# Differential attention on Trainium2: both maps' scores in one five-bank tile, a block's products with v in one bank

## The chip, the core and the metric

One Trainium2 chip, of which the program uses one core. The time is the device time of one execution of the whole program in microseconds (us); a kernel's figure is the median of several executions. The engines are PE (TensorE, matmuls; PEld is its loading of weights), DVE (VectorE), ACT (ScalarE), POOL (GpSimd) and SP (SyncE, which issues transfers). Matmuls write to PSUM, which has eight banks of 512 float32 columns over 128 partitions; DVE and ACT read it from there. The granted clock of PE is given as a share of its full 2.4 GHz: 1.00 is that level and 0.50 is 1.2 GHz.

## The reference

The program runs two layers of a hybrid model over 1024 latent tokens and 256 context tokens. In each layer one projection feeds three groups of heads (differential attention, windowed attention, a recurrent unit), whose outputs are joined by an output projection; a gated MLP follows. The change concerns differential attention alone. It has four heads with two maps each, of 32 dimensions, and values of 64:

```python
def attend(qb, keys, vals):
    s = jnp.einsum('bqhmd,bkhmd->bhmqk', qb, keys).astype(F32) * scale
    p = jax.nn.softmax(s, axis=-1)
    w = p[:, :, 0] - lam * p[:, :, 1]
    return jnp.einsum('bhqk,bkhd->bqhd', w.astype(vals.dtype), vals)
```

Latent queries see all 1280 keys, context queries (layer 0 only) the 256 keys of the context. The result is normalised per head.

## The kernel before

`phase_b` (L699) runs windowed attention and then `da` (L860), once per layer. `da` works through units: a head of one pair of heads, with a block of query tiles of 128 tokens (four tiles of latents, or the two context tiles). Each tile of a unit is a step. Layer 0 has 40 steps, of which 32 are long (1280 keys) and 8 short (256 keys); layer 1 has 32 long ones. So there are 72 steps and 144 maxima.

A long step does, for each of the two maps: three score matmuls into a PSUM tile of three banks (512, 512 and 256 columns, L901, `da_s`), the negated maximum over the keys on DVE (L911), and the exponential with its sum on ACT (L918, `da_e`; the sum is read out by a second instruction, ACTIVATION_READ_ACCUMULATOR). `combine` then forms the weights of both maps on DVE: a reciprocal (L929), a small product (L930), and one wide operation that adds the scaled map 1 to map 0 (L931). Ten transposes on PE (L942, `da_t`) follow, in groups of 4, 4 and 2, which ACT copies out (L943, `da_w`, two of 512 columns and one of 256), and ten pairs' worth of products with v (`pv_mm`, L742, `da_pv`), which use the upper and lower half of the partitions in turn. `pv_combine` (L744) adds the halves: a copy on ACT (L749, `pvt`) and an addition on DVE (L750, `da_o`), once for each step. After a block's second head, `sub_norm` normalises it in three instalments.

Eight PSUM banks are shared out as follows: the pool psD has two buffers of a score tile (six banks), so that the two maps of a step have one each; the pool of `ps_t` has two banks, which transposes, products with v and all fill work take in turn.

Fill work stands between the steps. `fill_plan` (L1008) spreads over them parts of the output projection (`piece`: nine matmuls of 426, 428 or 342 columns, L1048 to L1050, `oy_ps`; a scaled copy on ACT, L1054, `oy_z`; an addition on POOL, L1056) and of the modulation of later stages (`mod_units`: matmuls L302, a copy on ACT L330, transposes L291, sums on DVE L293 and L296). There are 24 pieces in either layer.

The kernel states operations in a written order, but a scheduler sets the order on each engine when the program is built, and sees to the waits; where a PSUM tile is concerned it does so by banks. In each engine the instructions then run in that order. The source of `da` states for step n: combination n−1, products n−2, the maxima and exponentials of n, `finish` n−2, fill, the scores of n+1 with the transposes n−1 between the two maps.

Of the kernel before, what the change touches and what calls it, by code (L numbers as in the profile page):

```python
# [11 lines left out]
F32 = mybir.dt.float32  # L12
F32R = mybir.dt.float32r
AF = mybir.ActivationFunctionType
ALU = mybir.AluOpType
AX = mybir.AxisListType
PSUM = bass.MemoryType.PSUM
# [4 lines left out]
P = 128  # L22
NLAT = 1024
NCTX = 256
T = NLAT + NCTX
# [145 lines left out]
class Build:  # L171
# [527 lines left out]
    def phase_b(self):  # L699
        nc, tc = self.nc, self.tc  # L700
        with ExitStack() as st:
            self.sp = st.enter_context(tc.tile_pool(name="sB", bufs=1))
            self.s5_bufs = 6
            todo = [(1, nb) for nb in range(6, 12)] if self.last else \
                [(0, nb) for nb in range(4, 12)] + [(1, nb) for nb in range(6)]
            self.lambdas()
            with tc.tile_pool(name="psS", bufs=3, space=PSUM) as pss:
                v = self.load_v(256)
                loaded = [self.sw_in, self.sw_load(1, "h")]
                for g in range(2):  # L710
                    self.sw(pss, v, *loaded[g], g)
            with tc.tile_pool(name="psD", bufs=2, space=PSUM) as pss:
                self.da(pss, todo)

    def lambdas(self):
# [144 lines left out]
    def da(self, pss, todo):  # L860

        nc, sp = self.nc, self.sp
        loaded = [{}, {}]
        self.yh, self.yl, self.ld = {}, {}, {}

        def load(pair, ms):
            if 0 in ms:
                loaded[pair]["v"] = self.load_v(P * pair)  # L870
            for m in ms:
                loaded[pair][m] = self.da_load(pair, m)

        load(0, (0, 1))
        load(0, (2, 3))
        blocks = ([] if self.last else [([8, 9], 8)]) + [([0, 1, 2, 3], 0), ([4, 5, 6, 7], 0)]
        units = []
        for pair in range(2):
            bs = [dict(pair=pair, tiles=tiles, kt0=kt0, nk=10 - kt0, nkc=T - P * kt0, nqb=P * len(tiles))
                  for tiles, kt0 in blocks]  # L880
            for hd in range(2):
                for blk in bs:
                    units.append(dict(blk=blk, hd=hd))
        steps = [(u, ti) for u in units for ti in range(len(u["blk"]["tiles"]))]
        ns = len(steps)
        state = [dict(e=[], s=[None, None]) for _ in steps]
        plan = self.fill_plan(ns, todo)
        late = []

        def scores(n, mi):  # L890
            u, ti = steps[n]
            b = u["blk"]
            nkc = b["nkc"]
            t = b["tiles"][ti]
            tok = slice(P * t, P * t + P)
            qm, km = loaded[b["pair"]][2 * u["hd"] + mi]
            k0 = T - nkc
            s = state[n]["s"][mi] = pss.tile([P, T], F32, tag="s", name="da_s")
            for c in range(0, nkc, 512):
                w = min(512, nkc - c)  # L900
                nc.tensor.matmul(s[:, c:c + w], qm[:, tok], km[:, k0 + c:k0 + c + w], start=True, stop=True)  # L901

        def maximum(n, mi):
            u, ti = steps[n]
            st, b = state[n], u["blk"]
            if mi == 0:
                st["sm"] = sp.tile([P, 8], F32, tag="sm", name="da_sm", bufs=8)
                if u["hd"] == 0 and ti == 0:
                    b["s0"] = sp.tile([P, 4, 2, 2], F32, tag="s0", name="da_s0", bufs=5)
                    b["o"] = self.s5("da_o")  # L910
            nc.vector.tensor_reduce(st["sm"][:, mi:mi + 1], st["s"][mi][:, :b["nkc"]], AX.X, ALU.max, negate=True)  # L911

        def exps(n, mi):
            u, ti = steps[n]
            st, b = state[n], u["blk"]
            nkc = b["nkc"]
            e = self.x_tile("da_e")
            nc.scalar.activation(e[:, :nkc], st["s"][mi][:, :nkc], AF.Exp, bias=st["sm"][:, mi:mi + 1],  # L918
                                 accum_out=b["s0"][:, ti, u["hd"], mi:mi + 1])
            st["e"].append(e)  # L920

        def combine(n):

            u, ti = steps[n]
            st, b = state[n], u["blk"]
            sm, (w, e1) = st["sm"], st["e"]
            s01 = b["s0"][:, ti, u["hd"], :]
            nkc = b["nkc"]
            nc.vector.reciprocal(sm[:, 4:5], s01[:, 1:2])  # L929
            nc.vector.scalar_tensor_tensor(sm[:, 5:6], s01[:, 0:1], self.nlam, sm[:, 4:5], ALU.mult, ALU.mult)  # L930
            nc.vector.scalar_tensor_tensor(w[:, :nkc], e1[:, :nkc], sm[:, 5:6], w[:, :nkc], ALU.mult, ALU.add)  # L931

        def transpose(n):
            u, ti = steps[n]
            st, b = state[n], u["blk"]
            w = st["e"][0]
            wt = st["wt"] = self.wt_tile("da_w", F32)
            for c in range(0, b["nk"], 4):
                n4 = min(4, b["nk"] - c)
                pt = self.ps_t("da_t")  # L940
                for i in range(n4):
                    nc.tensor.transpose(pt[:, P * i:P * i + P], w[:, P * (c + i):P * (c + i) + P], self.ident)  # L942
                nc.scalar.activation(wt[:, P * c:P * (c + n4)], pt[:, :P * n4], AF.Copy)  # L943

        def products(n):
            u, ti = steps[n]
            st, b = state[n], u["blk"]
            hd, nk = u["hd"], b["nk"]
            pv = st["pv"] = self.ps_t("da_pv")[:, :P]
            for c in range(nk):  # L950
                self.pv_mm(pv, c, nk, loaded[b["pair"]]["v"][:, b["kt0"] + c, 64 * hd:64 * hd + 64],
                           st["wt"][:, P * c:P * c + P])

        def finish(n):
            u, ti = steps[n]
            b = u["blk"]
            self.pv_combine(u["hd"], state[n]["pv"], b["o"][:, P * ti:P * ti + P], P)
            if u["hd"] == 1 and ti == len(b["tiles"]) - 1:
                late.append(self.sub_norm(b))

        scores(0, 0)
        scores(0, 1)
        for n in range(ns + 2):
            if n == ns // 4 + 3:
                load(1, (0, 1))
            if n == ns // 2 + 3:
                load(1, (2, 3))
            if n == ns - 10:
                for k in range(2, KE):
                    self.y_load(k, "h")  # L970
            if n == ns - 4:
                self.y_split(2, nc.scalar, nc.gpsimd)
            if n == ns - 3:
                self.y_split(3, nc.scalar, nc.gpsimd)
            prev, new, out = 1 <= n <= ns, n + 1 < ns, n >= 2
            if prev:
                combine(n - 1)
            if out:
                products(n - 2)
            if n < ns:  # L980
                maximum(n, 0)
            if n < ns:
                exps(n, 0)
            if n < ns:
                maximum(n, 1)
            if n < ns:
                exps(n, 1)
            if out:
                finish(n - 2)
            if n < ns:  # L990
                for fn in plan[n]:
                    fn()
            if new:
                scores(n + 1, 0)
            if prev:
                transpose(n - 1)
            if new:
                scores(n + 1, 1)
            late = [g for g in late if next(g, True) is None]
            if n == ns - 2:  # L1000
                self.wo = [self.weight(self.a["wo"][self.l, 0], KE * P)]
        for fn in plan[ns]:
            fn()
        for g in late:
            for _ in g:
                pass
# [763 lines left out]
```

## Time and profile before

| | |
|---|---|
| median of the runs | 3106.06 us (3 runs: 3099.3, 3106.1, 3106.06) |
| the profiled execution | 3104.49 us, its span 3102.6 us |
| granted clock of PE, mean | 0.972 |
| busy over the whole span | PE 2845.3 us (92%), DVE 2109.1 (68%), ACT 1457.5 (47%) |
| maxima L911, 144 of them | 195.5 us busy |
| exponentials L918, 144 | 177.5 us busy |
| scores L901, 400 | 125.2 us busy |

The span is the time from the first to the last instruction of one execution. A row of the timeline gives an instruction's start, its duration, and in brackets how long the engine was idle before it and what ended that; a row marked x2 or more stands for instructions that ran without a gap. Differential attention takes from about 488 to 727 us in layer 0 and from 2121 to 2327 us in layer 1.

### The profile page before, as it was taken

How to read it: one execution, taken by the hardware profiler on the slowest of the kernel's cores; microseconds unless marked ns; L12 is line 12 of the kernel's file. 1: busy time of each engine (PE TensorE's matmuls, PEld its weight loads, DVE VectorE, ACT ScalarE, POOL GpSimd, SP SyncE). 2: the span in 40 equal slices, each digit the busy share in tenths (PEclk: the TensorE clock that was granted, in tenths of full speed). 3: DMA queues.
4: the chain of work that ended last, by engine and by line, in shares of the span. 5: the costliest groups of instructions: out<-in, count | busy, mean ns of one | idle time of the engine just before them, and what ended most of it. 6: DMA issues, size and time to landing. Idle time of an engine off the chain costs nothing. (4 is left out here: it accounts for less than half of the span.)

```text
span 3102.6 us, 41077 instructions
## 1 busy us (share of the span) xinstructions
PE 2845.3 (92%) x15194; PEld 2307.3 (74%) x15194; DVE 2109.1 (68%) x2979; ACT 1457.5 (47%) x2442; POOL 1497.3 (48%) x971
## 2 busy tenths in 40 slices
PE   6899798999899999998988989798989799998898
PEld 4798665667688888887877778666767678887676
DVE  6956577875855444457887875767885755555997
ACT  5444367775444333343322454467873444444331
POOL 4645402223455444439561664602323566665981
PEclk9999899999999999999999999899999999999999
DMA  7232816654121121143215331454434122224322
GB/s 251 83 93 68 202 27 228 204 197 149 59 80 67 67 75 67 67 174 118 82 57 206 92 108 52 123 121 146 134 110 166 55 82 82 82 82 163 121 84 82
DMA packets 207577, 349.27 MB, mean 113 GB/s; under 512 B 32784, under 2 KB 112400, under 8 KB 207376
## 3 DMA queue, kind: packets, MB, share of 16 engines
q1 hardware_dynamic: 202768, 331.69, 33.2%
q0 software_dynamic: 4608, 14.95, 2.2%
q8 instruction: 120, 1.97, 0.3%
q14 instruction: 81, 0.66, 0.1%
HBM read 257.19 MB, written 89.39 MB: 112 GB/s over the span
## 5 line engine op out<-in xcount | busy, mean ns | idle before, releaser
L184 ACT ACTIVATE w_r<-w_raw 128x512 fp32r<-128x512 f32 x338 | 212.7, 631 | 449.7 <-PE u_ps L1518 280.1
L1490 POOL TENSOR_TENSOR w_raw<-w_raw 128x512 f32<-128x512 f32 x176 | 250.3, 1427 | 227.5 <-DVE w_r L187 102.8
L187 DVE TENSOR_TENSOR w_r<-w_raw,w_r 128x512 fp32r<-128x512 f32 x206 | 150.4, 732 | 251.5 <-ACT w_r L184 251.4
L187 POOL TENSOR_TENSOR w<-raw,w 128x1024 fp32r<-128x1024 f32 (+2 forms) x62 | 142.9, 2311 | 318.2 <-ACT w L184 207.1
L1517 PE MATMUL u_ps<-a,w_r 128*128 128x512 f32 x704 | 278.6, 396 | 5.3 <-DVE vb L1605 4.2
L1518 PE MATMUL u_ps<-a,w_r 128*128 128x512 f32 x704 | 277.8, 395 | 1.4 <-DVE a L187 1.2
L1519 PE MATMUL u_ps<-a,w_r 128*128 128x512 f32 x704 | 276.2, 392 | 0.0
L187 POOL TENSOR_TENSOR w_r<-w_raw,w_r 128x512 fp32r<-128x512 f32 x132 | 190.4, 1442 | 119.9 <-ACT w_r L184 114.7
L1369 PE MATMUL d_ps<-d_ah,d_b 128*128 128x512 f32 x560 | 223.1, 399 | 22.5 <-DVE xd L1346 11.1
L1370 PE MATMUL d_ps<-d_al,d_b 128*128 128x512 f32 x560 | 222.8, 398 | 9.0 <-DVE d_al L187 9.0
L1371 PE MATMUL d_ps<-d_ah,d_b 128*128 128x512 f32 x560 | 221.8, 396 | 0.7 <-DVE d_b L187 0.7
L911 DVE TENSOR_REDUCE da_sm<-da_s 128x1 f32<-128x1280 f32 (+1 forms) x144 | 195.5, 1368 | 34.1 <-PE da_s L901 32.7
L918 ACT ACTIVATE da_e<-da_s,da_sm 128x1280 f32<-128x1280 f32 (+1 forms) x144 | 177.5, 1235 | 23.7 <-DVE da_sm L911 20.6
L1056 POOL TENSOR_TENSOR oy_x<-oy_x,oy_z 128x426 f32<-128x426 f32 (+3 forms) x48 | 52.7, 1099 | 223.5 <-ACT oy_z L1054 191.7
L1517 PEld LDWEIGHTS u_ps<-a,w_r 128*128 128x128 f32 x704 | 133.8, 190 | 35.0 <-DVE vb L1605 5.7
L1518 PEld LDWEIGHTS u_ps<-a,w_r 128*128 128x128 f32 x704 | 133.9, 190 | 29.5 <-DVE a L187 2.0
L1519 PEld LDWEIGHTS u_ps<-a,w_r 128*128 128x128 f32 x704 | 133.7, 190 | 28.7
L1346 DVE SCALAR_TENSOR_TENSOR xd<-d_ps,mods,xd 128x512 f32<-128x512 f32 x200 | 141.0, 740 | 20.4 <-PE d_ps L1371 20.3
L1369 PEld LDWEIGHTS d_ps<-d_ah,d_b 128*128 128x128 f32 x560 | 107.6, 192 | 48.5 <-issue 9.4
L901 PE MATMUL da_s<-dak,daq 96*128 96x512 f32 (+1 forms) x400 | 125.2, 399 | 17.6 <-ACT da_e L918 17.4
L1605 DVE TENSOR_TENSOR vb<-u_ps,vb 128x512 f32<-128x512 f32 x96 | 66.1, 688 | 98.7 <-PE u_ps L1519 89.1
L1370 PEld LDWEIGHTS d_ps<-d_al,d_b 128*128 128x128 f32 x560 | 108.0, 193 | 32.0 <-DVE d_al L187 10.3
(347 smaller groups left out, 8635.6 us busy)
## 6 DMA issues: line engine op xcount, KB each, us to landing
wmod<-in_wmod SPq DMA_DIRECT2D x96, 512.0 KB, 6.4
w_raw<-in_wu SPq DMA_DIRECT2D x44, 1024.0 KB, 5.4
d_w<-in_wd SPq DMA_DIRECT2D x40, 512.0 KB, 3.9
d_a<-ud SPq DMA_DIRECT2D x40, 512.0 KB, 4.7
ud<-conv SPq DMA_DIRECT2D x22, 640.0 KB, 2.9
ud<-conv SPq DMA_DIRECT2D x22, 512.0 KB, 2.6
raw<-in_wg SPq DMA_DIRECT2D x16, 512.0 KB, 4.3
dak<-qk_da POOLq DMA_DIRECT2D x48, 160.0 KB, 8.1
```

The lines of the kernel that those rows point to most:

```text
L184: self.nc.scalar.activation(out, in_, AF.Copy)
L187: (eng or self.nc.vector).tensor_tensor(out, in_, hi.bitcast(F32), ALU.subtract)
L911: nc.vector.tensor_reduce(st["sm"][:, mi:mi + 1], st["s"][mi][:, :b["nkc"]], AX.X, ALU.max, negate=True)
L918: nc.scalar.activation(e[:, :nkc], st["s"][mi][:, :nkc], AF.Exp, bias=st["sm"][:, mi:mi + 1], accum_out=b["s0"][:, ti, u["hd"], mi:mi + 1])
L1346: nc.vector.scalar_tensor_tensor(x, ps, gate, x, ALU.mult, ALU.add)
L1369: nc.tensor.matmul(ps, bh[:, w], ah[:, m], start=on is None and k == 0, stop=False, **kw)
L1370: nc.tensor.matmul(ps, bh[:, w], al[:, m], start=False, stop=False, **kw)
L1371: nc.tensor.matmul(ps, bl[:, w], ah[:, m], start=False, stop=k == 1, **kw)
L1490: sub = lambda o, a, b, op=ALU.subtract: nc.gpsimd.tensor_tensor(o, a, b, op)
L1517: nc.tensor.matmul(ps, wh[:, s], h, start=new and kk == 0, stop=False, skip_group_check=not new)
L1518: nc.tensor.matmul(ps, wh[:, s], lo, start=False, stop=False, skip_group_check=not new)
L1519: nc.tensor.matmul(ps, wl[:, s], h, start=False, stop=kk == 3, skip_group_check=not new)
```

## The change

The pool psD has one buffer instead of two, and holds two tiles. `both` has 2560 columns, which are five banks: map 0 in columns 0 to 1279, map 1 in columns 1280 to 2559. Its third bank (columns 1024 to 1535) holds the end of map 0 and the beginning of map 1. The score matmuls of map 1 are cut at 256 and 768 so that each stays in one bank. The tile `pv` is one bank, in which up to four tiles of a unit put their products with v, 128 columns each; `pv_combine` then runs once for each unit, over 256 or 512 columns: 20 times instead of 72. The source states the maxima and exponentials of step n ahead of combination n−1, `finish` ahead of the scores, and the scores in two parts around the fill.

```diff
@@ -709,7 +709,7 @@
                 loaded = [self.sw_in, self.sw_load(1, "h")]
                 for g in range(2):
                     self.sw(pss, v, *loaded[g], g)
-            with tc.tile_pool(name="psD", bufs=2, space=PSUM) as pss:
+            with tc.tile_pool(name="psD", bufs=1, space=PSUM) as pss:
                 self.da(pss, todo)
 
     def lambdas(self):
@@ -883,11 +884,16 @@
                     units.append(dict(blk=blk, hd=hd))
         steps = [(u, ti) for u in units for ti in range(len(u["blk"]["tiles"]))]
         ns = len(steps)
-        state = [dict(e=[], s=[None, None]) for _ in steps]
+        state = [dict(e=[]) for _ in steps]
+        both = pss.tile([P, 2 * T], F32, tag="s", name="da_s")
         plan = self.fill_plan(ns, todo)
         late = []
 
-        def scores(n, mi):
+        def score(n, mi):
+            b = steps[n][0]["blk"]
+            return both[:, T * mi:T * mi + b["nkc"]]
+
+        def scores(n, mi, parts):
             u, ti = steps[n]
             b = u["blk"]
             nkc = b["nkc"]
@@ -895,10 +901,12 @@
             tok = slice(P * t, P * t + P)
             qm, km = loaded[b["pair"]][2 * u["hd"] + mi]
             k0 = T - nkc
-            s = state[n]["s"][mi] = pss.tile([P, T], F32, tag="s", name="da_s")
-            for c in range(0, nkc, 512):
-                w = min(512, nkc - c)
-                nc.tensor.matmul(s[:, c:c + w], qm[:, tok], km[:, k0 + c:k0 + c + w], start=True, stop=True)
+            cuts = [0, 512, 1024, nkc] if mi == 0 else [0, 256, 768, nkc]
+            s = score(n, mi)
+            for i in parts:
+                c, e = cuts[i], min(cuts[i + 1], nkc)
+                if c < e:
+                    nc.tensor.matmul(s[:, c:e], qm[:, tok], km[:, k0 + c:k0 + e], start=True, stop=True)
 
         def maximum(n, mi):
             u, ti = steps[n]
@@ -908,14 +916,14 @@
                 if u["hd"] == 0 and ti == 0:
                     b["s0"] = sp.tile([P, 4, 2, 2], F32, tag="s0", name="da_s0", bufs=5)
                     b["o"] = self.s5("da_o")
-            nc.vector.tensor_reduce(st["sm"][:, mi:mi + 1], st["s"][mi][:, :b["nkc"]], AX.X, ALU.max, negate=True)
+            nc.vector.tensor_reduce(st["sm"][:, mi:mi + 1], score(n, mi), AX.X, ALU.max, negate=True)
 
         def exps(n, mi):
             u, ti = steps[n]
             st, b = state[n], u["blk"]
             nkc = b["nkc"]
             e = self.x_tile("da_e")
-            nc.scalar.activation(e[:, :nkc], st["s"][mi][:, :nkc], AF.Exp, bias=st["sm"][:, mi:mi + 1],
+            nc.scalar.activation(e[:, :nkc], score(n, mi), AF.Exp, bias=st["sm"][:, mi:mi + 1],
                                  accum_out=b["s0"][:, ti, u["hd"], mi:mi + 1])
             st["e"].append(e)
 
@@ -946,7 +954,9 @@
             u, ti = steps[n]
             st, b = state[n], u["blk"]
             hd, nk = u["hd"], b["nk"]
-            pv = st["pv"] = self.ps_t("da_pv")[:, :P]
+            if ti == 0:
+                u["pv"] = pss.tile([P, 512], F32, tag="pv", name="da_pv")
+            pv = u["pv"][:, P * ti:P * ti + P]
             for c in range(nk):
                 self.pv_mm(pv, c, nk, loaded[b["pair"]]["v"][:, b["kt0"] + c, 64 * hd:64 * hd + 64],
                            st["wt"][:, P * c:P * c + P])
@@ -954,12 +964,13 @@
         def finish(n):
             u, ti = steps[n]
             b = u["blk"]
-            self.pv_combine(u["hd"], state[n]["pv"], b["o"][:, P * ti:P * ti + P], P)
-            if u["hd"] == 1 and ti == len(b["tiles"]) - 1:
-                late.append(self.sub_norm(b))
-
-        scores(0, 0)
-        scores(0, 1)
+            if ti == len(b["tiles"]) - 1:
+                self.pv_combine(u["hd"], u["pv"], b["o"], b["nqb"])
+                if u["hd"] == 1:
+                    late.append(self.sub_norm(b))
+
+        for mi in range(2):
+            scores(0, mi, range(3))
         for n in range(ns + 2):
             if n == ns // 4 + 3:
                 load(1, (0, 1))
@@ -973,29 +984,26 @@
             if n == ns - 3:
                 self.y_split(3, nc.scalar, nc.gpsimd)
             prev, new, out = 1 <= n <= ns, n + 1 < ns, n >= 2
+            if n < ns:
+                maximum(n, 0)
+                exps(n, 0)
+                maximum(n, 1)
+                exps(n, 1)
             if prev:
                 combine(n - 1)
             if out:
                 products(n - 2)
-            if n < ns:
-                maximum(n, 0)
-            if n < ns:
-                exps(n, 0)
-            if n < ns:
-                maximum(n, 1)
-            if n < ns:
-                exps(n, 1)
-            if out:
                 finish(n - 2)
+            if new:
+                scores(n + 1, 0, (0, 1))
             if n < ns:
                 for fn in plan[n]:
                     fn()
             if new:
-                scores(n + 1, 0)
+                scores(n + 1, 0, (2,))
+                scores(n + 1, 1, range(3))
             if prev:
                 transpose(n - 1)
-            if new:
-                scores(n + 1, 1)
             late = [g for g in late if next(g, True) is None]
             if n == ns - 2:
                 self.wo = [self.weight(self.a["wo"][self.l, 0], KE * P)]
```

How the emitted order changes. In these rows a name ending in a number is one of several buffers; the number behind [waits ...] is that of a semaphore, and the word ahead of it the engine or queue waited for (Activation is ACT).

On DVE, in long steps of layer 0, before (da_s_4447 are the sums of the exponentials):

```order
L931 SCALAR_TENSOR_TENSOR da_e<-da_e,da_sm 128x1280 [waits DVE_49]
L911 TENSOR_REDUCE da_sm<-da_s 128x1 [waits PE_49]
L929 RECIPROCAL da_sm<-da_s_4447 128x1 [waits Activation_49]
L750 TENSOR_TENSOR da_o<-da_pv,pvt 64x128 [waits Activation_49]
L930 SCALAR_TENSOR_TENSOR da_sm<-da_s_4447,nlam,da_sm 128x1 [waits DVE_49]
L911 TENSOR_REDUCE da_sm<-da_s 128x1 [waits PE_49]
L931 SCALAR_TENSOR_TENSOR da_e<-da_e,da_sm 128x1280 [waits DVE_49]
L911 TENSOR_REDUCE da_sm<-da_s 128x1 [waits PE_49]
```

The same place now:

```order
L919 TENSOR_REDUCE da_sm<-da_s 128x1 [waits PE_49]
L919 TENSOR_REDUCE da_sm<-da_s 128x1 [waits Activation_49]
L937 RECIPROCAL da_sm<-da_s_4409 128x1 [waits Activation_49]
L938 SCALAR_TENSOR_TENSOR da_sm<-da_s_4409,nlam,da_sm 128x1 [waits DVE_49]
L939 SCALAR_TENSOR_TENSOR da_e<-da_e,da_sm 128x1280 [waits DVE_49]
L919 TENSOR_REDUCE da_sm<-da_s 128x1 [waits PE_49]
L919 TENSOR_REDUCE da_sm<-da_s 128x1 [waits Activation_49]
```

Before, a maximum waited for PE only, and stood behind a combination in one step and ahead of it in another. Now each step reads maximum, maximum, reciprocal, product, combination; the second maximum waits for ACT. No addition into da_o (L750) stands among them.

On PE, in long steps of layer 0, before (dak and daq are keys and queries of one map):

```order
L942 MATMUL da_t<-cst_all,da_e 128x128 [waits DVE_49]
L942 MATMUL da_t<-cst_all,da_e 128x128 x3
L901 MATMUL da_s<-dak_4065,daq_4064 128x512 x2
L901 MATMUL da_s<-dak_4065,daq_4064 128x256
L901 MATMUL da_s<-dak_4057,daq_4056 128x512 [waits Activation_49]
L942 MATMUL da_t<-cst_all,da_e 128x128 [waits Activation_49]
L942 MATMUL da_t<-cst_all,da_e 128x128 x3
L942 MATMUL da_t<-cst_all,da_e 128x128 [waits Activation_49]
L942 MATMUL da_t<-cst_all,da_e 128x128
L901 MATMUL da_s<-dak_4057,daq_4056 128x512
L901 MATMUL da_s<-dak_4057,daq_4056 128x256
L742 MATMUL da_pv<-da_w,v 64x128 [waits Activation_49]
```

Now:

```order
L909 MATMUL da_s<-dak_4057,daq_4056 128x512 [waits Activation_49]
L909 MATMUL da_s<-dak_4057,daq_4056 128x512
L909 MATMUL da_s<-dak_4057,daq_4056 128x256
L909 MATMUL da_s<-dak_4065,daq_4064 128x256
L909 MATMUL da_s<-dak_4065,daq_4064 128x512 x2
L950 MATMUL da_t<-cst_all,da_e 128x128 [waits DVE_49]
L950 MATMUL da_t<-cst_all,da_e 128x128 x3
L950 MATMUL da_t<-cst_all,da_e 128x128 [waits Activation_49]
L950 MATMUL da_t<-cst_all,da_e 128x128 x3
L950 MATMUL da_t<-cst_all,da_e 128x128 [waits Activation_49]
L950 MATMUL da_t<-cst_all,da_e 128x128
L742 MATMUL da_pv<-da_w,v 64x128 x4
```

Before, the scores of one map ran without a wait of their own and those of the other waited for ACT, with transposes between them. Now the first of six waits for ACT, and all six stand together ahead of the transposes.

On ACT, in a long step of layer 0 with a piece of the output projection, now:

```order
L951 ACTIVATE da_w<-da_t 128x512 [waits PE_49,Activation_49]
L951 ACTIVATE da_w<-da_t 128x512 [waits PE_49]
L926 ACTIVATE da_e,da_s_4409<-da_s,da_sm 128x1280 [waits DVE_49,Activation_49]
L951 ACTIVATE da_w<-da_t 128x256 [waits PE_49]
L1062 ACTIVATE oy_z<-oy_ps,mods_85 128x428 [waits PE_49,Pool_49]
L926 ACTIVATE da_e,da_s_4409<-da_s,da_sm 128x1280 [waits DVE_49]
L951 ACTIVATE da_w<-da_t 128x512 [waits PE_49,Activation_49]
L951 ACTIVATE da_w<-da_t 128x512 [waits PE_49]
```

Ahead of a step's first exponential stand two copies of transposes; between it and the second, which waits for DVE alone, stand the third copy and oy_z. There is an oy_z at that place in 12 long steps of layer 0 and 19 of layer 1.

## Rows read from the trace of the kernel before

**Rows 1.** Windows: the two stretches of differential attention; columns as in the header.
```profile
core 0: us, PE busy (x) PEld busy (x) DVE busy (x) ACT busy (x) POOL busy (x), PEclk, DMA share, GB/s
488.00:727.00 239.00, 218.70 (x1662) 158.83 (x1660) 189.30 (x274) 183.37 (x353) 69.27 (x60) 0.98 0.60 190
2121.00:2327.00 206.00, 182.49 (x1487) 142.55 (x1486) 171.59 (x218) 166.34 (x299) 62.53 (x60) 0.98 0.46 136
sum 445.00, PE 401.20 PEld 301.38 DVE 360.89 ACT 349.71 POOL 131.81; mean PE 200.60 PEld 150.69 DVE 180.44 ACT 174.85 POOL 65.90
```

**Rows 2.** Timeline of DVE, layer 1: start us, us busy, then the instruction.
```profile
2145.88 2.88 DVE L911 TENSOR_REDUCE da_sm<-da_s 128x1 f32<-128x1280 f32 x2
...
2149.59 1.55 DVE L931 SCALAR_TENSOR_TENSOR da_e<-da_e,da_sm 128x1280 f32<-128x1280 f32 x1
2151.05 2.88 DVE L911 TENSOR_REDUCE da_sm<-da_s 128x1 f32<-128x1280 f32 x2
```

**Rows 3.** Timeline of DVE: first and last step of layer 0, then of layer 1.
```profile
488.48 1.49 DVE L911 TENSOR_REDUCE da_sm<-da_s 128x1 f32<-128x1280 f32 x1
...
721.12 1.49 DVE L911 TENSOR_REDUCE da_sm<-da_s 128x1 f32<-128x1280 f32 x1 [0.22 <-PE da_s L901]
...
2121.70 1.49 DVE L911 TENSOR_REDUCE da_sm<-da_s 128x1 f32<-128x1280 f32 x1
...
2320.40 1.49 DVE L911 TENSOR_REDUCE da_sm<-da_s 128x1 f32<-128x1280 f32 x1
```

**Rows 4.** Waits, 484:775 (layer 0): who waits <- for whom: us in total, times, longest.
```profile
DVE da_sm L911 <- PE da_s L901: 19.9, 22, 2.1
...
PEld da_s L901 <- ACT da_e L918: 14.6, 18, 2.1
```

**Rows 5.** Groups by form, 484:740: count, busy us, mean ns, idle before.
```profile
L911 DVE TENSOR_REDUCE da_sm<-da_s 128x1 f32<-128x1280 f32 x64 | 94.7, 1487 | 16.4 <-PE da_s L901 15.7
...
L943 ACT ACTIVATE da_w<-da_t 128x512 f32<-128x512 f32 x64 | 37.2, 597 | 10.2 <-PE da_t L942 10.0
...
L943 ACT ACTIVATE da_w<-da_t 128x256 f32<-128x256 f32 x40 | 15.4, 385 | 2.5 <-PE da_t L942 2.2
...
L750 DVE TENSOR_TENSOR da_o<-da_pv,pvt 64x128 f32<-64x128 f32 x40 | 11.5, 287 | 11.5 <-ACT pvt L749 10.1
...
L749 ACT ACTIVATE pvt<-da_pv 64x128 f32<-64x128 f32 x40 | 10.8, 271 | 11.1 <-PE da_pv L742 10.4
...
L1054 ACT ACTIVATE oy_z<-oy_ps,mods 128x426 f32<-128x426 f32 x8 | 4.9, 612 | 4.6 <-PE oy_ps L1050 4.6
```

**Rows 6.** Timeline of DVE and of ACT, layer 0: a maximum and its exponential.
```profile
607.31 1.49 DVE L911 TENSOR_REDUCE da_sm<-da_s 128x1 f32<-128x1280 f32 x1 [1.20 <-PE da_s L901]
...
608.90 1.33 ACT L918 ACTIVATE da_e<-da_s,da_sm 128x1280 f32<-128x1280 f32 x1 [1.30 <-DVE da_sm L911]
610.12 0.19 ACT L918 ACTIVATION_READ_ACCUMULATOR da_e<-da_s,da_sm 128x1 f32 x1
```

**Rows 7.** Timeline of DVE, layer 0: from a reciprocal to the next maximum.
```profile
619.46 0.17 DVE L929 RECIPROCAL da_sm<-da_s 128x1 f32<-128x1 f32 x1
...
621.50 1.49 DVE L911 TENSOR_REDUCE da_sm<-da_s 128x1 f32<-128x1280 f32 x1
```

**Rows 8.** Timeline of PE, layer 0.
```profile
613.46 1.73 PE L942 MATMUL da_t<-cst_all,da_e 128*128 128x128 f32 x10
...
618.07 0.46 PE L1048 MATMUL oy_ps<-oy_h,w 128*128 128x426 f32 x1
...
619.93 0.40 PE L901 MATMUL da_s<-dak,daq 96*128 96x512 f32 x1
...
620.30 1.22 PE L901 MATMUL da_s<-dak,daq 96*128 96x512 f32 x5
```

**Rows 9.** Windows of 4 us, columns as in rows 1.
```profile
2132.00:2136.00 4.00, 1.32 (x7) 1.04 (x8) 1.50 (x2) 3.86 (x6) 2.37 (x1) 1.00 0.83 258
...
720.00:724.00 4.00, 4.00 (x18) 3.49 (x16) 2.61 (x8) 2.03 (x5) 1.67 (x1) 0.50 0.00 0
```

## The prediction

> **What bounds the kernel now.** I read the windows first. The two stretches in which differential attention runs last 445 us together, and neither TensorE (401.2 us busy), nor VectorE (360.9), nor ScalarE (349.7) fills them [rows 1]: three engines stand close to each other, and what links them decides. The timeline of VectorE gives the rhythm. In layer 1 the pair of maxima of one step starts at 2145.88 and that of the next at 2151.05: 5.17 us, two maxima without a gap between them (2.88 us) and one combination [rows 2]. That is the best rhythm. From the first maximum of the first step to that of the last, layer 1 takes 2320.40 − 2121.70 = 198.7 us for 31 intervals, **6.41 us a step**; layer 0 takes 721.12 − 488.48 = 232.64 us for 37 intervals, 6.29 us, six short steps of 256 keys among them [rows 3]. I take 6.41 for each of the 64 long steps (1280 keys), 410 us in all; the short ones I leave aside. The 1.24 us above the best rhythm is fill work getting in between. In the waits of layer 0, a maximum waits for its scores 19.9 us in all, and the weight loads of the scores for an exponential 14.6 us [rows 4]: small against 239 us, because each map has its own score tile and there are two. A map's scores can be written while the other map is read.
>
> **The change, part by part.**
>
> *One tile for both maps.* Map 0 has columns 0 to 1279, map 1 columns 1280 to 2559; columns 1024 to 1535 are one bank, which both maps use, and there is no second tile. The emitted order says what becomes of it: map 1's maximum now waits on ScalarE, for map 0's exponential, in all 72 steps, where it waited for TensorE; the next step's first score matmul waits for map 1's exponential in 70 of 71 steps, and both maps' six matmuls stand behind it. The combination stands on VectorE ahead of the next step's first maximum in each step, though the source now writes the maxima ahead of it. So four operations that overlapped become a chain: maximum 0, exponential 0, maximum 1, exponential 1, and then the next step.
>
> Its length by rows: a maximum is 1.487 us [rows 5]; from its start to the start of the exponential that uses it 608.90 − 607.31 = 1.59 us; from there to the end of the read of its sum 610.12 + 0.19 − 608.90 = 1.41 us [rows 6]. From the reciprocal through the combination to the next maximum: 621.50 − 619.46 = 2.04 us [rows 7]. Chain: 2.04 + 2 × (1.59 + 1.41) = 8.04 us. The new hand-over from exponential 0 to maximum 1 has no row in this trace; between nothing and the 0.10 us by which 1.59 exceeds a maximum, I take 0.03. With that, **8.07 us**. The next step's scores hide: five matmuls are 1.22 us [rows 8], so six about 1.45, beside 2.04 us of combination. Should that cover go (if the combination stood elsewhere), they would cost their 1.45.
>
> *ScalarE's queue on that chain.* The copies of the transposes (two of 0.597 us, one of 0.385 [rows 5]) used to lie anywhere. Now the two long ones stand ahead of exponential 0. With the chain's start at 0: combination done at 2.04, maximum 0 until 3.56, but the transposes can only begin at 2.1. Ten of them are 1.73 us [rows 8], four about 0.6; so the copies run from 2.7 to 3.9, and exponential 0 begins at 3.95, not at 3.63: 0.3 us, giving **8.4 us**. The copy of 256 columns runs beside maximum 1 and costs nothing.
>
> *Fill pieces.* In 31 of the 64 long steps (12 in layer 0, 19 in layer 1) the copy of an output piece (oy_z) stands between the two exponentials. Its nine matmuls are split around the last two products with v, which wait for the copy of 256 columns. That copy ends at about 5.75, the two products at 6.05. Of the nine matmuls (619.93 − 618.07 = 1.86 us [rows 8]) the later half, about 0.95, then ends at 7.0, and the copy, 0.61 us [rows 5], at 7.65, where maximum 1 was done at 6.88. Exponential 1 starts at 7.7 instead of 6.98, 0.7 us late: **9.1 us** in layer 0. Layer 1's pieces have 342 columns instead of 426; at four fifths the late part (0.95 + 0.61 = 1.56 us) is about 0.25 less: 8.85.
>
> *Products of a block in one bank.* The additions into da_o fall from 72 to 20 and so do the copies beside them. A copy is 0.271 us and an addition 0.287 [rows 5], wider ones at most 0.6 by the row of the 512-column copy; 52 fewer saves at most 52 × 0.29 = 15 us on either engine. VectorE waits inside the new chain, so I count nothing. If the chain were not the bound, the 15 us would be the gain's upper end.
>
> *Matmul cuts.* Six a step as before, with borders at 256 and 768 for map 1: nothing.
>
> *Sum.* 12 × 9.1 + 19 × 8.85 + 33 × 8.4 = 554.6 us for 64 steps, against 410.2: +144. Other ScalarE work that may land between the exponentials (a finished block's normalisation, ten blocks with some three copies of about 0.6 each, a third of them in the way) I put at +6. TensorE now pauses: 6.3 us of work a step (401.2 / 64) in 8.7. The clock has been at 1.00 in a stretch where TensorE was busy 1.32 of 4 us, yet at 0.50 in another, where it was busy all 4 us [rows 9]. For more stretches of the second kind I put +8, an estimate: four of them, each costing half of its 4 us. Total **+158 us**: 3104.5 + 158 = 3262.5 for the profiled execution, which lies 1.6 below the median of the runs shown, so **3264 us**.
>
> *A rule against this change.* Row and order say that the readers of one bank, and not the scores, cost most. The Trainium skill, "Perfetto Trace Analysis", section "Matmuls" under "Optimizing Tensor Performance", says that independent matmul groups should rotate through different banks, so that evacuating one overlaps the matmuls of the next. By that rule alone the loss would be the scores' 1.45 us in each of 64 steps, +93, 3199 us; by the rows these matmuls hide beside the combination, and the loss lies elsewhere.
>
> **The rivals.**
>
> *The bare chain* (0.18). The copies and pieces find their places beside the maxima, as they do in the best rhythm of before. Then 64 × 8.07 = 516.5, +106, and 3212 us. For it: VectorE has 5.0 us of work in 8 then (two maxima and 2.04), and ScalarE idles too. Against it: the queues are in order, and the copies stand where they stand.
>
> *The clock falls for long* (0.17). If TensorE is at 0.50 for a quarter of the steps, its 6.3 us become 12.5, which no longer fit into 8.7: 16 × 3.8 = +61, 3325 us. For it: pauses of about 2 us come in every step. Against it: the clock at 1.00 with 1.32 of 4 us busy, and 0.98 as the mean of both stretches [rows 1, 9]. The Trainium skill, "TensorE: Matmul & The Clock Gate", section "A second HAM failure mode: psum-queue depth-cycling", reports a kernel whose pauses between groups of matmuls made the clock swing; the stretch at 0.50 [rows 9] agrees with it as far as one stretch goes.
>
> *The other side: faster* (0.03). The chain is no bound if each step's links take less than 6.41 us together. Then what decides is TensorE's idle time, 445 − 401.2 = 44 us, of which the removed additions and copies could free a part, 15 us at most by the above: about 3091. It would need the rows' chain of 8.07 to be a quarter too long, though each of its durations comes from a row.
>
> *The change does not do what it says* (0.02 for no difference). The maxima are not ahead of the combination in the emitted order. If VectorE nevertheless got past it, the chain would be 6 us plus 1.45 for the scores, 7.5, and +70, 3176 us; no difference at all would need the shared bank not to bind. I leave the 7.5 us case at 0.03, below the range.
>
> **How the numbers follow.** My forecast, 8.4 to 9.1 us a step, has 0.57. Its own error of 0.4 us a step is 26 us: 3238 to 3290. The range takes in the bare chain, less 7, and the falling clock, plus 13: **3205 to 3338**. A measurement can tell about 0.3%, 9 us, from no change. Faster 0.03, same 0.02, slower 0.95.
>
> **What would show it.** In the profile after: maximum 1 waits for exponential 0 in each step (waits of VectorE for da_e of some 1.4 us × 64 or more); first maxima some 8.4 us apart, 9 where oy_z stands between the exponentials; VectorE's busy share in these stretches near 60%; scores begin right behind exponential 1 and end ahead of the combination. A mean step below 8 us would show the chain wrong; one of 10 or more, or a granted clock below 0.9 over these stretches, the clock rival; a mean under 6.4 everything.

## The result: 3347 us, 7.8% slower

The changed kernel takes 3347.16 us (median of 4 runs, 3338.7 to 3352.21) against 3104.98 us; the ratio is 1.0776, with a 95% interval of 1.0756 to 1.0796. The direction and the chain were forecast, the size was not: 3347 lies 83 us above the forecast and 9 us above the range.

The page of the profile after:

```profile
span 3350.2 us, 41003 instructions
...
PE 2987.0 (89%) x15194; PEld 2375.5 (71%) x15194; DVE 2092.0 (62%) x2927; ACT 1452.0 (43%) x2390; POOL 1491.7 (45%) x971
...
L919 DVE TENSOR_REDUCE da_sm<-da_s 128x1 f32<-128x1280 f32 (+1 forms) x144 | 197.2, 1369 | 125.0 <-ACT da_e L926 102.5
...
L926 ACT ACTIVATE da_e<-da_s,da_sm 128x1280 f32<-128x1280 f32 (+1 forms) x144 | 177.0, 1229 | 34.4 <-DVE da_sm L919 32.9
...
L909 PE MATMUL da_s<-dak,daq 96*128 96x512 f32 (+1 forms) x400 | 112.2, 418 | 67.9 <-ACT da_e L926 67.9
```

DVE did 17 us less work than before and ACT 6 us less (the copies and additions that the change removes), and PE was busy 142 us longer for the same matmuls: part of it ran at the lower clock. What ends the maxima's idle time is no longer PE but ACT, with 102.5 us. The line of the page before:

```profile
L911 DVE TENSOR_REDUCE da_sm<-da_s 128x1 f32<-128x1280 f32 (+1 forms) x144 | 195.5, 1368 | 34.1 <-PE da_s L901 32.7
```

The windows from the first long step's maximum to the last one's, of either layer, then of two single steps:

```profile
498.54:837.73 339.19, 268.46 (x1648) 176.18 (x1649) 180.57 (x244) 176.80 (x321) 66.78 (x60) 0.89 0.41 129
2242.19:2565.25 323.06, 251.68 (x1475) 176.90 (x1474) 163.18 (x189) 160.39 (x271) 60.25 (x60) 0.79 0.29 86
2281.22:2290.26 9.04, 7.48 (x56) 3.96 (x56) 5.77 (x9) 5.16 (x9) 2.47 (x5) 1.00 0.37 102
2373.97:2388.45 14.48, 12.37 (x55) 9.49 (x56) 4.98 (x6) 5.26 (x9) 2.57 (x2) 0.52 0.09 25
```

339.19 and 323.06 us stand where 232.64 and 198.7 stood [rows 3]: 230.9 of the 247.6 us by which the span grew; 10 more come ahead of the first long step. Layer 1 has 10.42 us a step instead of 6.41. The granted clock is 0.89 and 0.79, where it was 0.98 [rows 1]. The two last rows are one step at the full clock, 9.04 us, and one at a clock of 0.52, 14.48 us, the longest of all.

The timeline of a step with a piece of the output projection at the full clock, DVE and ACT (start us, us, then the instruction):

```profile
2272.12 1.48 DVE L919 TENSOR_REDUCE da_sm<-da_s 128x1 f32<-128x1280 f32 x1
...
2274.07 1.32 ACT L926 ACTIVATE da_e<-da_s,da_sm 128x1280 f32<-128x1280 f32 x1
...
2275.38 0.38 ACT L951 ACTIVATE da_w<-da_t 128x256 f32<-128x256 f32 x1
...
2275.52 1.49 DVE L919 TENSOR_REDUCE da_sm<-da_s 128x1 f32<-128x1280 f32 x1 [1.91 <-ACT da_e L926]
...
2277.41 0.55 ACT L1062 ACTIVATE oy_z<-oy_ps,mods 128x342 f32<-128x342 f32 x1 [1.65 <-PE oy_ps L1058]
2277.85 1.32 ACT L926 ACTIVATE da_e<-da_s,da_sm 128x1280 f32<-128x1280 f32 x1
...
2279.06 0.20 ACT L926 ACTIVATION_READ_ACCUMULATOR da_e<-da_s,da_sm 128x1 f32 x1
2279.30 0.16 DVE L937 RECIPROCAL da_sm<-da_s 128x1 f32<-128x1 f32 x1 [2.29 <-ACT da_e L926]
...
2279.75 1.55 DVE L939 SCALAR_TENSOR_TENSOR da_e<-da_e,da_sm 128x1280 f32<-128x1280 f32 x1
...
2281.22 1.48 DVE L919 TENSOR_REDUCE da_sm<-da_s 128x1 f32<-128x1280 f32 x1
```

This is the forecast's chain link by link in one of the shorter steps: maximum at 2272.12, exponential at 2274.07, the second maximum as that ends (2275.52, 1.91 us of DVE idle), then oy_z at 2277.41 in the way, the second exponential at 2277.85, the combination, the next maximum at 2281.22: 9.10 us, where 8.85 was forecast for layer 1.

And the waits of layer 0 (who waits <- for whom: us in total, times, longest):

```profile
DVE da_sm L937 <- ACT da_e L926: 48.0, 26, 4.1
DVE da_sm L919 <- ACT da_e L926: 46.7, 27, 2.8
...
ACT oy_z L1062 <- PE oy_ps L1058: 34.0, 18, 4.3
DVE mods L293 <- PE mod_t L291: 33.5, 12, 5.7
...
DVE da_sm L919 <- PE da_s L909: 11.6, 15, 1.6
```

A maximum now waits 46.7 us for an exponential and 11.6 for its scores (19.9 before [rows 4]). DVE also waits 33.5 us for the transposes of a modulation unit (L291); layer 1 adds 11.2. The forecast has no term for that.

### The profile page after: what moved, and what is told of

Same layout as the page of the kernel before. It is cut to its first block, busy times and chain, and to the rows that moved or that the text cites. A ratio compares the mean times of both kernels' runs of the same rounds, so it can differ in the third digit from the quotient of the medians.

```text
span 3350.2 us, 41003 instructions
## 1 busy us (share of the span) xinstructions
PE 2987.0 (89%) x15194; PEld 2375.5 (71%) x15194; DVE 2092.0 (62%) x2927; ACT 1452.0 (43%) x2390; POOL 1491.7 (45%) x971
## 5 line engine op out<-in xcount | busy, mean ns | idle before, releaser
L919 DVE TENSOR_REDUCE da_sm<-da_s 128x1 f32<-128x1280 f32 (+1 forms) x144 | 197.2, 1369 | 125.0 <-ACT da_e L926 102.5
L950 PE MATMUL da_t<-cst_all,da_e 128*128 128x128 f32 x656 | 130.9, 351 | 67.2 <-DVE da_e L939 53.1
L951 ACT ACTIVATE da_w<-da_t 128x512 f32<-128x512 f32 (+1 forms) x200 | 100.9, 520 | 168.1 <-PE da_t L950 167.5
L950 PEld LDWEIGHTS da_t<-cst_all,da_e 128*128 128x128 f32 x656 | 95.7, 177 | 109.8 <-issue 44.6
L909 PE MATMUL da_s<-dak,daq 96*128 96x512 f32 (+1 forms) x400 | 112.2, 418 | 67.9 <-ACT da_e L926 67.9
```

Of the source, the lines that this page charges most:

```text
L919: nc.vector.tensor_reduce(st["sm"][:, mi:mi + 1], score(n, mi), AX.X, ALU.max, negate=True)
```

## The experiments

Two theories stood at first. **A**, the prediction's: the third bank, which both maps use, makes the second maximum wait for the first exponential. **B**: the waits follow the tile, whatever banks are read. A is what the text ahead of the prediction says of the scheduler ("by banks"). **C** is that something else in the change (the order of the source, the products' bank) made the loss.

**e1, one tile of six banks**

```diff
-        both = pss.tile([P, 2 * T], F32, tag="s", name="da_s")
+        both = pss.tile([P, 3072], F32, tag="s", name="da_s")
-            return both[:, T * mi:T * mi + b["nkc"]]
+            return both[:, 1536 * mi:1536 * mi + b["nkc"]]
-            cuts = [0, 512, 1024, nkc] if mi == 0 else [0, 256, 768, nkc]
+            cuts = [0, 512, 1024, nkc]
```

with the products in a tile for each step, as before the change.

> One tile of six banks: map 1 begins at column 1536, so no bank holds both maps; products with v go back to the other pool, a tile for each step. Theory A (the prediction's: two readers of one bank make the chain): with no shared bank the second maximum needn't wait for the first exponential, so steps fall to about 6.4 to 6.6 us and the time to 3105 to 3130 us. Rival B (the waits follow the tile, whichever banks are read): the second maximum and all six scores still wait, so steps stay near 10 us and the time within 25 us of the change's 3347; 52 more copies and additions are worth at most 15 us of that.

**e2, two tiles of three banks**

```diff
-        both = pss.tile([P, 2 * T], F32, tag="s", name="da_s")
+        two = [pss.tile([P, T], F32, tag=f"s{mi}", name="da_s") for mi in range(2)]
-            return both[:, T * mi:T * mi + b["nkc"]]
+            return two[mi][:, :b["nkc"]]
```

with the cuts and products of e1.

> Two tiles of three banks, one for each map, one buffer each; products with v as in e1; the order of the source is the change's. Theories A and B both: each map's scores and maximum wait only for their own tile, steps 6.4 to 6.6 us, granted clock of both stretches back to 0.97 or more, 3105 us within 20. Rival C (it is the order of the source, or the products' bank, that made the loss): over 3150 us.

**e3, the change with a product tile for each step**

```diff
-            if ti == 0:
-                u["pv"] = pss.tile([P, 512], F32, tag="pv", name="da_pv")
-            pv = u["pv"][:, P * ti:P * ti + P]
+            pv = st["pv"] = self.ps_t("da_pv")[:, :P]
```

> The change's one tile of five banks, but a product tile for each step in the other pool, as before. Theories A and B: the chain of maxima and exponentials stays and hides the rest, so within 15 us of 3347. Rival C: if the products' bank made the loss, the time falls towards 3105; if it had hidden a gain, it rises by up to 15 us (52 times 0.29).

Measured: e1 3288.81 us (ratio to before 1.0588, interval 1.057 to 1.0606), e2 3107.4 (1.0007, 0.9993 to 1.0021), e3 3283.0 (1.0571, 1.0553 to 1.0589). The waits of e1, then of e2, in layer 0:

```profile
DVE da_sm L919 <- ACT da_e L926: 44.6, 30, 3.1
...
DVE da_sm L919 <- PE da_s L909: 14.1, 13, 4.1
```

```profile
DVE da_sm L919 <- PE da_s L909: 19.3, 17, 3.0
```

In e1 no bank holds both maps, and the maximum still waits 44.6 us for the exponential; in e2 that wait is gone, and with it the whole loss. **A falls, B stands**: it is the one tile, not the shared bank. What the text ahead of the prediction says, that the scheduler sees to the waits of a PSUM tile by banks, is too narrow for e1. e1 lies under B's 25 us around 3347 because of what e3 shows: e3 has the change's five banks and the change's chain, and yet takes 64 us less. So the part of the change that gives the products a bank, to which the forecast gave nothing, costs 64 us; e1 and e3, with shared bank or without, are 6 us apart. C falls for the order of the source (e2) and holds in part for the products' bank.

**e4, the combination behind both maxima**

```diff
+            nl = self.nlam
+            if n + 1 < ns:
+                nl = sm[:, 6:7]
+                nc.vector.scalar_tensor_tensor(nl, state[n + 1]["sm"][:, 1:2], 0.0, self.nlam, ALU.mult, ALU.add)
...
-            nc.vector.scalar_tensor_tensor(sm[:, 5:6], s01[:, 0:1], self.nlam, sm[:, 4:5], ALU.mult, ALU.mult)
+            nc.vector.scalar_tensor_tensor(sm[:, 5:6], s01[:, 0:1], nl, sm[:, 4:5], ALU.mult, ALU.mult)
```

> The change, with one small operation added in each step's combination that reads the next step's second maximum, so that the combination runs behind both maxima, beside the second exponential and the scores. Chain theory: a step is 1.45 (scores) + 2 x (1.59 + 1.41) + 0.03 = 7.5 us in place of 8.07 at the full clock, so about 0.6 us less in 64 steps: some 3310 us, if ScalarE's copies fall no worse. Rival D (the clock of TensorE and the fill set the step, the chain hides in it): no change, 3347 within 10.

Measured: 3320.19 us (1.0697, 1.0672 to 1.0722), 27 us under the change and 10 over the 3310 of the chain theory; D's "no change" falls. With what the change says of itself, maxima ahead of the combination, really done, the single tile keeps most of the loss. The 27 us are no pure price of that order: 46 copies oy_z stand between the exponentials, in 42 long steps instead of 31, and the matmuls of only 4 of the 48 pieces are split around products with v, where the change splits 36.

**Why do the products cost 64 us?** In the change oy_z stands between the two exponentials in 31 long steps, in e3 in 5: where the products don't take one of the two banks of the other pool in turn, a piece's matmuls are split around the last products (36 of 48 pieces in the change, none in e3), and its copy falls into the chain. The likely reason, that a piece gets its bank earlier there, is argued and not shown. e5 brings oy_z out of the chain and keeps the products' bank; e6 keeps the bank for products alone, but combines each step.

**e5, a dry run of the products**

```diff
-            for c in range(nk):
+            for c, nk in [(k, min(8, b["nk"])) for r in range(1) for k in range(min(8, b["nk"]))] + [(k, b["nk"]) for k in range(b["nk"])]:
```

> The change, with the first eight tiles of keys multiplied with v twice: a dry run of 16 matmuls ahead of the real 20, which start the sum anew, so the result is the same. It adds about 16 x 0.065 = 1.05 us of TensorE work to each long step (67 us in all), and in the emitted order the piece's copy (oy_z) now stands between the two exponentials in 5 long steps instead of 31, as in e3; the products' bank stays as in the change. Theory P (what the products' bank costs is this place of oy_z, and the lower clock that goes with longer steps): 3265 to 3290 us, in spite of the added work. Rival Q (the bank itself is waited for): 3347 or more. Rival R (TensorE's work sets the step): up to 3347 + 67.

**e6, the products' bank for one step at a time**

```diff
-            if ti == 0:
-                u["pv"] = pss.tile([P, 512], F32, tag="pv", name="da_pv")
-            pv = u["pv"][:, P * ti:P * ti + P]
+            pv = st["pv"] = pss.tile([P, 512], F32, tag="pv", name="da_pv")[:, :P]
```

and, as in e3, a combination in each step.

> The change, with the products' bank kept for products alone, but taken anew and combined in each step (72 copies and additions again). In the emitted order oy_z stands between the exponentials in 32 long steps and the small copy beside it in 58. Theory P: near the change, 3340 to 3370 us. Rival Q (fewer, wider combinations make the loss, for the next block's products wait for them): towards 3283, as e3.

Measured: e5 3273.69 us (1.0554, 1.0536 to 1.0572), e6 3331.43 (1.0744, 1.0725 to 1.0763). Q and R fall: e5 adds some 67 us of TensorE work to the change and is 73 us faster. P's range for e5 holds. e6 lies 9 us under P's range and far from Q's 3283; its 52 more copies and additions cost nothing that shows. The pieces agree: e6 splits 37 of 48 around products, e5 only 4.

But P is not shown to be all of it. The orders of e3 and e5 also shorten DVE's wait for the modulation's transposes, which P leaves out. In layer 0 it is 33.5 us in the change and 25.4 in e6; here are its lines of e3, then of e5:

```profile
DVE mods L293 <- PE mod_t L291: 20.0, 10, 5.9
```

```profile
DVE mods L293 <- PE mod_t L291: 12.0, 7, 5.3
```

And long steps of layer 0 at the full clock (0.95 or more in the step's own window) that have no oy_z between their exponentials still take 9.43 us in the change (mean of 11) and 8.61 in e3 (of 22). Which of these makes how much of the 64 us is open.

**e7, the modulation's transposes first**

```diff
+            if late:
+                self.mod_out(*late)
             for k in range(KC):
                 self.mod_mm(ps, k, raws[k // 2][:, 512 * (k % 2):512 * (k % 2) + 512], k < 4, k >= 4)
...
             nc.scalar.activation(m, ps, AF.Copy)
-            if late:
-                self.mod_out(*late)
```

> The change, with the transposes and sums of a modulation unit stated ahead of the next unit's sixteen matmuls instead of behind them. In the change VectorE waits 33.5 + 11.2 us for those transposes, ahead of a reciprocal, mostly on the chain. If the wait goes: 3300 to 3325 us. Rival: the sums stand ahead of the reciprocal as before and wait for something else that is as late: 3347 within 10.

Measured: 3324.61 us (1.0715, 1.0699 to 1.0732), 22.6 under the change, at the upper end of the range. The wait of DVE that this edit aims at, in layer 0 (33.5 us in the change):

```profile
DVE mods L293 <- PE mod_t L291: 8.5, 4, 3.9
```

With 1.0 us in layer 1, 44.7 us of waits have become 9.5, and the time fell by 22.6 of these 35.

**e8, e3 with two dry runs**: e5's edit on e3, with `range(2)`.

> e3 with two dry runs of 16 matmuls in each step: 2.1 us of TensorE work more a long step, 134 us in all, the result the same. TensorE's work at the full clock is then 6.3 + 2.1 = 8.4 us a step, still under e3's 8.6 to 8.9 us at that clock. Clock theory (pauses of TensorE bring the clock down, and with it part of the loss): the granted clock of the two stretches rises from 0.93 and 0.87 to 0.95 or more, and the time stays within 20 us of 3283. Rival (the clock doesn't follow the pauses, or TensorE's work binds): clock as in e3 and 3330 us or more.

Measured: 3278.06 us (1.0564, 1.0548 to 1.0579). The windows from the first long step's maximum to the last one's, of e3 and then of e8:

```profile
497.65:805.05 307.40, 240.27 (x1648) 163.75 (x1646) 185.30 (x271) 180.12 (x348) 70.92 (x60) 0.94 0.45 142
2205.92:2497.32 291.40, 221.76 (x1475) 160.26 (x1474) 174.72 (x212) 162.43 (x294) 66.96 (x60) 0.88 0.33 95
```

```profile
498.86:823.22 324.36, 286.33 (x2624) 219.93 (x2622) 184.41 (x271) 180.69 (x347) 64.84 (x60) 0.96 0.42 133
2223.97:2489.93 265.96, 234.36 (x2387) 189.71 (x2387) 174.82 (x212) 164.45 (x293) 67.12 (x60) 0.99 0.36 102
```

TensorE has 976 matmuls more in layer 0 and 912 in layer 1, and the program takes no longer (the intervals of the two overlap). In layer 1 the clock goes from 0.88 to 0.99 and the stretch from 291 to 266 us, 9.40 to 8.58 us a step; in layer 0 the clock goes from 0.94 to 0.96, and the added work shows: 17 us more. The clock theory's signs came. But the order differs between the two (oy_z stands between the exponentials in 15 long steps instead of 5), and layer 1's wait of DVE for the modulation's transposes fell from 6.3 us to 1.1, so the 25 us of layer 1 are not the clock's alone.

**e9, both maxima ahead of both exponentials**

```diff
                 maximum(n, 0)
-                exps(n, 0)
                 maximum(n, 1)
+                exps(n, 0)
                 exps(n, 1)
```

> The change, with both maxima of a step stated ahead of both exponentials. The tile is the same, so the next scores still wait for the second exponential; the second maximum no longer waits, but the first exponential now waits for it. In the emitted order no copy stands between the two exponentials in any long step, and the three copies of the transposes stand ahead of the first, which starts late enough for them. Chain theory: 2.04 + 1.49 + 1.45 + 0.10 + 2 x 1.41 = 7.9 us a step at the full clock, 64 x (7.9 - 6.45) = 93 us over before, and 20 to 40 us for a lower clock: 3215 to 3240 us. Rival (one of the two waits alone, the second maximum's for the first exponential, made the loss): under 3150 us. Rival (the single tile's loss is the clock's and the fill's): over 3270 us.

Measured: 3264.07 us (1.0522, 1.0492 to 1.0552), 83 us under the change, which is the largest gain of one edit that keeps the tile. The rival by which the second maximum's wait alone made the loss falls: the wait is gone and 159 us of loss are left. At the full clock (each step's own window, clock 0.95 or more) a step takes 8.07 us in layer 0 and 8.56 in layer 1, where 7.9 was expected; part of layer 1's excess is shown in the last section. The range of 3215 to 3240 was missed by 24 us. The second rival, that the loss is the clock's and the fill's, set its bound at 3270, and 3264 is too near to it to rule it out: the clock of the two stretches was 0.90 and 0.87.

**e10 and e11, a version that beats both?** e7's edit on the kernel before, and on e2.

> The kernel before with e7's edit alone. There VectorE waits for the transposes of a modulation unit 6.6 + 3.1 us in the two stretches, not all of it on a path that ends last: 0 to 8 us faster, most likely 4. Rival: those waits are hidden, no change.

> e2 (two tiles, the change's order of the source) with e7's edit: as e10, 0 to 8 us under e2's 3107.

Measured: 3103.23 us (0.9991, 0.9981 to 1.0002) and 3104.73 (1.0003, 0.9991 to 1.0015). Neither can be told from the kernel before: where the maps have their own tiles, those waits are hidden. Nothing tried here beats the kernel before.

## Why the prediction was wrong in size

**The chain was right, its cause was not.** Maximum, exponential, maximum, exponential, combination run one behind the other, as forecast, and without the chain nothing of the loss is left (e2). But the step "columns 1024 to 1535 are one bank, which both maps use" failed as a cause: e1 has no such bank and the same waits. The sum didn't hang on it, for the forecast read the waits from the emitted order; that the right chain came with the wrong reason is luck. The rule of the Trainium skill that was weighed ("Perfetto Trace Analysis", "Matmuls": rotate through different banks) doesn't reach that either. In e1 each map has its own three banks, and one tile undoes them.

**The copies of the transposes were right.** From maximum 0 to exponential 0 the forecast had 3.95 − 2.07 = 1.88 us; the timeline shows 2274.07 − 2272.12 = 1.95, and the mean over the 24 long steps at the full clock (below) is 1.98.

**"Products of a block in one bank: I count nothing" failed.** The saved copies are worth nothing, as said. But the same part of the change sets where the pieces fall, and that was costed as a fact of the order, 12 × 0.7 + 19 × 0.45 = 17 us, and not as this part's price. (A fifth of the late 1.56 us is 0.31, not 0.25; over 19 steps that is 1 us.) Against e3 the part costs 64 us. A piece's copy in the chain makes TensorE's work part of the chain: at the lower clock its matmuls are late, and the second exponential waits for them. The timeline of the step at 0.52 shows it:

```profile
2373.97 1.49 DVE L919 TENSOR_REDUCE da_sm<-da_s 128x1 f32<-128x1280 f32 x1
...
2376.23 1.32 ACT L926 ACTIVATE da_e<-da_s,da_sm 128x1280 f32<-128x1280 f32 x1
...
2378.76 1.48 DVE L919 TENSOR_REDUCE da_sm<-da_s 128x1 f32<-128x1280 f32 x1
...
2384.01 0.55 ACT L1062 ACTIVATE oy_z<-oy_ps,mods 128x342 f32<-128x342 f32 x1 [2.76 <-PE oy_ps L1058]
2384.45 1.32 ACT L926 ACTIVATE da_e<-da_s,da_sm 128x1280 f32<-128x1280 f32 x1
```

The second maximum is done at 2380.24, and oy_z begins at 2384.01: 3.8 us in which the second exponential waits for the piece; for 2.76 of them ACT is idle until TensorE has done its matmuls.

**A wait was missing.** The sums of a modulation unit stand ahead of a reciprocal and wait for transposes: 22.6 us (e7). Before, the same wait was 6.6 + 3.1 us, and hidden (e10). It lies in the link from the second exponential to the next maximum, for which the forecast had 1.41 + 2.04 = 3.45 us: over the 24 steps at the full clock that link takes 3.94 on average.

**The clock was mis-sized.** With each step's own window, 24 of the 62 long steps of the two stretches had a clock of 0.95 or more, on average 9.65 us in layer 0 and 9.16 in layer 1; the forecast's means were 8.66 and 8.67, so the full-clock terms were short by 32 × 0.99 + 32 × 0.49 = 47 us (the missing wait among them). The other 38 steps were longer than these means by 47 us together, an estimate, where the forecast had +8. 3264 + 47 + 39 = 3350. The 64 us of the products' bank lie within these terms and are no further one: reckoned in the same way, e3's steps at the full clock are 40 us shorter, and its others lose 25 us instead of 47. The rival "the clock falls for long" gave 3325 with a chance of 0.17. The sign that the prediction set for it, a clock below 0.9 over these stretches, is there; it came about beside the forecast's chain, together with longer links, and not in place of them. Pauses of TensorE go with the lower clock here: 0.98 before, 0.89 and 0.79 with the longer steps; and the other way round in layer 1 of e8, where more work went with 0.99 instead of 0.88. That agrees with the Trainium skill, "TensorE: Matmul & The Clock Gate", section "A second HAM failure mode: psum-queue depth-cycling", which reports a kernel whose short pauses between groups of matmuls made the clock swing.

**What stays open.** How the 64 us of the products' bank divide into oy_z's place, the modulation's wait and the lower clock that comes with both (by the estimate above some 40 us are longer steps at the full clock), and how much of the clock's loss would be left in a chain without pieces in it. No run had the shorter chain and a full clock throughout.

## What to carry to other kernels

Two buffers that are read by different engines should be two tiles: in one tile their readers and writers wait for one another, though they touch other banks (e1). When an edit shortens nothing on the critical path, look at what it does to the order of the rest: which copy it lets fall between two links of a chain, and whether TensorE's work becomes a link. And where a chain makes TensorE pause, count its matmuls at the lower clock too.

## What was not expected of the hardware

A combination takes 1.55 us on DVE [rows 2], but at times 2.2 to 2.3. The timeline of e9, DVE and POOL, in two steps of layer 1:

```profile
2298.95 1.55 DVE L939 SCALAR_TENSOR_TENSOR da_e<-da_e,da_sm 128x1280 f32<-128x1280 f32 x1
...
2299.68 1.59 POOL L1064 TENSOR_TENSOR oy_x<-oy_x,oy_z 128x342 f32<-128x342 f32 x1 [2.15 <-ACT oy_z L1062]
...
2306.61 2.30 DVE L939 SCALAR_TENSOR_TENSOR da_e<-da_e,da_sm 128x1280 f32<-128x1280 f32 x1
2306.64 0.92 POOL L1064 TENSOR_TENSOR oy_x<-oy_x,oy_z 128x342 f32<-128x342 f32 x1 [5.37 <-ACT oy_z L1062]
```

In the first step the combination runs when GpSimd's addition begins, and the addition takes 1.59 us instead of 0.92. In the second both begin within 0.03 us, the addition takes its 0.92 us and the combination 0.75 us more. The Trainium skill, "SBUF — State Buffer", section "SBUF: two separate sides", says that VectorE's operations with two inputs from SBUF and GpSimd's share a pair of ports, which one of them holds for its whole instruction. The trace agrees, save that by the recorded starts the combination came first in the second case. In e9 13 of 64 long combinations took over 1.7 us, 9 us more than the usual 1.55 in all; in the change 4 did.

Then, that a program can gain by work for nothing: e5 runs some 67 us more of matmuls than the change and is 73 us faster, with a better order and a clock of 0.99 and 0.93 instead of 0.89 and 0.79. Its windows, as those of the change above:

```profile
498.12:795.60 297.48, 256.92 (x2156) 183.87 (x2153) 180.10 (x244) 175.35 (x321) 68.30 (x60) 0.99 0.45 147
2204.98:2487.40 282.42, 232.56 (x1953) 177.76 (x1951) 170.84 (x190) 158.77 (x271) 64.73 (x60) 0.93 0.33 98
```
